# Two sums over 512 elements against one over 1024: the modulation rows on VectorE in a two-layer diffusion step

## The chip, the cores and the metric

The kernel runs on one core of a Trainium2 chip. The metric is the device time of one execution in microseconds, the median of several runs. A profile is one execution taken by the hardware profiler; its times count from the start of its span.

## What is computed

The reference takes 128 context tokens and 512 latent tokens of width 1024 through two layers. Each layer is a mixer (pooling and short convolution in layer 0, attention in layer 1) and a gated feed-forward network, and ahead of both stands a normalisation whose shift, scale and gate come from a condition vector, one for the context, one for the latents:

```python
def ada_params(cvec, w_ada, b_ada):
    m = jax.nn.silu(cvec) @ w_ada + b_ada
    return jnp.split(m[:, None, :], 6, axis=-1)

def modulate(x, g, shift, scale):
    return rms_norm(x, g) * (1 + scale) + shift

for l in range(DEPTH):
    sh1, sc1, g1, sh2, sc2, g2 = ada_params(cond, w_ada[l], b_ada[l])
    h = modulate(x, norm_g[l, 0], sh1, sc1)
    x = x + g1 * mixer(h)
    h = modulate(x, norm_g[l, 1], sh2, sc2)
    x = x + g2 * swiglu(h, w_ffn_in[l], w_ffn_out[l])
```

For each layer `ada_params` is a product of the two conditions, after a SiLU, with a matrix of 1024 by 6144. The result is 6144 modulation values for each condition and layer, which the kernel calls rows: 128 of them, one for each partition, make a block, so there are 48 blocks for each layer.

## The kernel before, in words

Everything is kept transposed: features on the 128 partitions, the 640 tokens along the free axis. All large products run on TensorE as three products of a high and a low part (`block_mm`, line 287, two halves of 320 tokens each). The low parts are made by VectorE: `pair` rounds on ScalarE (L142) and subtracts on VectorE (L143), for weights (`wl_...`, 128x1024) and for activations (`al`, `bl`).

The modulation values of layer 0's first norm, and some others, are made by TensorE (`ada_pe`). The other 84 blocks are made on VectorE by the class `AdaDve`. For one block it loads the 128 rows of the transposed matrix (`rawa`, 128x1024), and for each of the two conditions multiplies them by that condition (`silb`, the same on all partitions) and sums along the row. Before the change this is done in two halves of 512 elements, by one operation each (L365), which writes the products to a tile that nobody reads (`junk`, one buffer) and the sum to one column of `got`. So a block costs four such operations. The profile shows each as two instructions: the operation itself (CUSTOM_DVE_ANT_0) and a read of its sum (DVE_READ_ACCUMULATOR2_ANT). When a group of four or eight blocks is done, one addition (L379) joins the two halves and `ada_done` adds the bias (L386).

The order of the work. The startup, up to about 60 us, is in an order written out by hand (`manual_schedule`): two calls `ada.run(2)`, so four blocks, stand there on VectorE's queue with one weight split between them (`ws.split(2)`), ahead of the end of the first normalisation (`rsqrt_of`, L448 to L460), for which TensorE then waits. Behind it come, in this order:

- the input projection of layer 0 (`pi`, 16 products, the last 13 with `each=` calling `ada.run` for two, one or no blocks), with the pooled branch (GpSimd sums at L878, VectorE at L888 and L889), the convolution (L935 to L969) and the evacuation of each product (L505, then L510 on ScalarE, which frees the PSUM tile);
- the output projection (`po`, 8 products, one block each), with the residual update of x (L490), the operand of the next norm (`prep`, L467 on ScalarE and L469 on VectorE) and the sum of squares (L422 on ScalarE, added on GpSimd at L424); at its end `rsqrt_of` splits the sum (`bl<-ssq_a`) and TensorE reduces it (L453);
- the feed-forward network of layer 0 (`fi`, `fo`), one block for each product until all 84 are done, at 612 us;
- layer 1, which has no such blocks.

Outside the startup a planner with a model of costs puts each engine's instructions in order before the run, and at run time each engine takes them strictly in that order. The sums are kept behind what stands before them in the program (`keep_in_program_order`), but others may be put between them. GpSimd adds tensors in the stages up to 245 us; both it and VectorE read them from SBUF. All loads go through SyncE's queue, a block's rows as one transfer of 512 KB, up to six ahead.

Of the kernel before, what the change touches and what calls it, by code (L numbers as in the profile page):

```python
# [9 lines left out]
F32 = mybir.dt.float32  # L10
F32R = mybir.dt.float32r
AF = mybir.ActivationFunctionType
ALU = mybir.AluOpType
AX = mybir.AxisListType

P = 128
D = 1024
# [41 lines left out]
def hybrid_step(  # L59
# [23 lines left out]
    V, S, G, PE = nc.vector, nc.scalar, nc.gpsimd, nc.tensor  # L83
# [18 lines left out]
    def tmp(name):  # L102
        return tpool.tile([P, UL], F32, tag="t", name=name)
# [233 lines left out]
    class AdaDve:  # L337
# [13 lines left out]
        def run(self, rows, hold=True):  # L351
            for _ in range(rows):
                if self.at == len(self.todo):
                    return
                l, b0, n, b = self.todo[self.at]
                if not self.raw:
                    self.load()
                raw = self.raw.pop(0)
                self.at += 1
                if b == 0:  # L360
                    self.got = p1.tile([P, 8, 2, 2], F32, tag="got", bufs=2, name=f"got_{l}_{b0}")
                for c in range(2):
                    for q in range(2):
                        cols = slice(512 * q, 512 * q + 512)
                        op = V.tensor_tensor_reduce(  # L365
                            out=junk,
                            in0=raw[:, cols],
                            in1=silb[:, c, cols],
                            scale=1.0,
                            scalar=0.0,  # L370
                            op0=ALU.mult,
                            op1=ALU.add,
                            accum_out=self.got[:, b, c, q : q + 1],
                        )
                        if hold:
                            tc.keep_in_program_order(op)
                if b == n - 1:
                    two = self.got[:, 0:n]
                    V.tensor_tensor(out=two[:, :, :, 0], in0=two[:, :, :, 0], in1=two[:, :, :, 1], op=ALU.add)  # L379
                    ada_done(l, b0, two[:, :, :, 0])  # L380
                self.load()

    def ada_done(l, b0, got):

        n = got.shape[1]
        V.tensor_tensor(  # L386
            out=mod[l][:, b0 : b0 + n, :],
            in0=got,
            in1=sm[:, S_BA + 48 * l + b0 : S_BA + 48 * l + b0 + n, None].broadcast_to((P, n, 2)),
            op=ALU.add,  # L390
        )
        part, k0 = divmod(b0, 8)
        if part in (1, 4):
            g0 = S_NG + 8 * (2 * l + part // 3) + k0
            V.scalar_tensor_tensor(
                out=sc[l, part // 3][:, k0 : k0 + n, :],
                in0=mod[l][:, b0 : b0 + n, :],
                scalar=1.0,
                in1=sm[:, g0 : g0 + n, None].broadcast_to((P, n, 2)),
                op0=ALU.add,  # L400
                op1=ALU.mult,
            )
        known.add((l, part, k0 + n))
# [319 lines left out]
    nc.sync.dma_start(sm, small)  # L723
    with tc.tile_pool(name="pool1", bufs=1) as p1:
        silb = p1.tile([P, 2, D], F32, tag="silb", name="silb")
        junk = p1.tile([P, 512], F32, tag="junk", name="junk")
        ada_raw = []

        def ada_load(ch):
# [297 lines left out]
    with tc.tile_pool(name="pool2", bufs=1) as p2:  # L1027
# [14 lines left out]
        for dst, srcd, nm in ((kt, ckT, "ck"), (vt, cv, "cv")):  # L1042
            raw = tmp(f"raw_{nm}")
# [511 lines left out]
```

## Time and profile before

| | |
|---|---|
| median of 3 runs | 1409.69 us (1408.79 to 1410.6) |
| the profiled execution | 1408.83 us, its span 1406.9 |
| mean granted TensorE clock | 0.983 |
| sums on VectorE (L365) | 336, together 250.5 us, the last at 612 us |
| reads of their sums | 336, 81 ns each |
| additions of the halves (L379) | 11 |
| loads of rows | 84 of 512 KB, 3.5 us from issue to landing |

Rows of the profile give a line, an engine and an operation, then the tile written and the tiles read, with their shapes; "idle before" names what ended the engine's wait. TensorE's busy time is modelled from pipelined matmuls. A granted clock of 1.00 is full speed; the other state seen here is 0.50, so that a mean of 0.82 over 5 us means that 36% of it ran at half speed. The span is the time from the first to the last instruction of the execution.

### The profile page before, as it was taken

Reading aid. Unit: us, or ns where it says so; the run is one execution under the profiler, and the core shown is the slowest. Engines: PE = TensorE matmul, PEld = TensorE weight load, DVE = VectorE, ACT = ScalarE, POOL = GpSimd, SP = SyncE. Lnnn points to the kernel's source line nnn. Section 1 sums busy time; section 2 is a strip of 40 time slices with the busy share of each in tenths; the row PEclk is TensorE's granted clock in tenths of the full one; section 3 lists DMA queues with packets and bytes.
Section 4 is the critical chain, followed back from the end, with each engine's and each line's share of the span. In section 5 each row is a group of like instructions: output and inputs, shape, how many; then the busy total and the mean of one; then the engine's idle time right before and its main releaser. Section 6 shows DMA issues by size and latency. Waiting matters only on the chain.

```text
span 1406.9 us, 22549 instructions
## 1 busy us (share of the span) xinstructions
PE 1361.5 (97%) x9139; PEld 1332.9 (95%) x9139; DVE 1006.5 (72%) x1955; ACT 578.1 (41%) x1025; POOL 148.4 (11%) x116
## 2 busy tenths in 40 slices
PE   6989998999999999999999999999999999999995
PEld 3889998999999999999999899999999999999995
DVE  4899999777768787754667677778973477536745
ACT  3433334332112221232465676547652255414543
POOL 3351112000000000000203221020000000000003
PEclk7999999999999999999999999999999999999998
DMA  9634544434343534221232111012132122311212
GB/s 363 248 106 153 184 150 157 152 135 165 135 165 122 176 123 168 87 90 46 91 110 93 46 46 39 31 44 77 41 111 91 32 89 90 121 61 61 76 46 75
DMA packets 36728, 154.50 MB, mean 110 GB/s; under 512 B 3984, under 2 KB 11152, under 8 KB 26000
## 3 DMA queue, kind: packets, MB, share of 16 engines
q1 hardware_dynamic: 36624, 153.07, 31.2%
q8 instruction: 71, 1.16, 0.3%
q14 instruction: 33, 0.27, 0.1%
HBM read 147.55 MB, written 2.88 MB: 107 GB/s over the span
## 4 chain that ended last, share of the span: by engine, by line
PE 78%; DVE 16%; issue 2%; ACT 2%; DMA 1%; POOL 1%; SPq 0%; DVEq 0%; POOLq 0%; ACTq 0%
PE fi L287 26%; PE fo L287 21%; PE fi L610 16%; DVE junk L365 6%; PE pq L287 5%; PE wa L287 2%; DVE al L469 2%; PE o L1289 2%; PE s L1239 1%; DVE wl_in L143 1%; PE t L1272 1%; DVE x L490 1%; DVE wl_out L143 1%; DVE bl L143 1%; DMA raw_ada<-wada 1%
## 5 line engine op out<-in xcount | busy, mean ns | idle before, releaser
L365 DVE CUSTOM_DVE_ANT_0 junk<-rawa,silb 128x512 f32<-128x512 f32 x336 | 250.5, 746 | 7.6 <-ACT silb L793 1.0
L287 PE MATMUL fi<-al,wh_fi 128*128 128x320 f32 x832 | 192.2, 312 | 2.2 <-DVE al L469 2.2
L287 PE MATMUL fi<-ah,wh_fi 128*128 128x320 f32 x832 | 192.5, 313 | 1.4 <-ACT ah L467 1.4
L287 PE MATMUL fi<-ah,wl_fi 128*128 128x320 f32 x832 | 191.6, 312 | 0.0
L490 DVE SCALAR_TENSOR_TENSOR x<-fo,mod,x 128x128 f32<-128x128 f32 (+1 forms) x144 | 54.6, 433 | 136.5 <-PE fo L287 133.1
L287 PEld LDWEIGHTS fi<-al,wh_fi 128*128 128x128 f32 x832 | 141.7, 190 | 2.8 <-DVE al L469 2.8
L287 PEld LDWEIGHTS fi<-ah,wh_fi 128*128 128x128 f32 x832 | 141.7, 191 | 1.6 <-ACT ah L467 1.6
L287 PEld LDWEIGHTS fi<-ah,wl_fi 128*128 128x128 f32 x832 | 141.4, 190 | 0.0
L142 ACT ACTIVATE wh_fi<-raw_fi 128x1024 fp32r<-128x1024 f32 x52 | 55.0, 1058 | 172.0 <-PE fi L287 134.8
L142 ACT ACTIVATE wh_fi_p<-raw_fi 128x512 fp32r<-128x512 f32 x126 | 77.3, 627 | 111.8 <-PE fi L610 65.0
L142 ACT ACTIVATE wh_fo<-raw_fo 128x1024 fp32r<-128x1024 f32 (+1 forms) x48 | 47.5, 991 | 180.5 <-PE fo L287 132.6
L143 DVE TENSOR_TENSOR wl_fi_p<-raw_fi,wh_fi_p 128x512 fp32r<-128x512 f32 x126 | 85.6, 688 | 48.5 <-ACT wh_fi_p L142 48.2
L610 PE MATMUL fi<-bh,wl_fi_p 128*128 128x320 f32 x288 | 88.9, 309 | 0.0
L610 PE MATMUL fi<-bh,wh_fi_p 128*128 128x320 f32 x288 | 88.7, 308 | 0.0
L610 PE MATMUL fi<-bl,wh_fi_p 128*128 128x320 f32 x288 | 88.3, 307 | 0.0
L287 PE MATMUL fo<-bh,wh_fo 128*128 128x320 f32 x352 | 80.6, 310 | 0.0
L287 PE MATMUL fo<-bh,wl_fo 128*128 128x320 f32 x352 | 80.5, 310 | 0.0
L287 PE MATMUL fo<-bl,wh_fo 128*128 128x320 f32 x352 | 80.4, 310 | 0.0
L424 POOL TENSOR_TENSOR ssq_b<-ssq_b,sq_b 128x640 f32<-128x640 f32 x14 | 25.2, 1801 | 516.6 <-ACT sq_b L422 516.5
L287 PE MATMUL fo<-al,wh_fo 128*128 128x320 f32 x328 | 75.1, 310 | 0.0
L287 PE MATMUL fo<-ah,wh_fo 128*128 128x320 f32 x328 | 74.9, 309 | 0.0
L287 PE MATMUL fo<-ah,wl_fo 128*128 128x320 f32 x328 | 74.8, 309 | 0.0
(342 smaller groups left out, 3317.1 us busy)
## 6 DMA issues: line engine op xcount, KB each, us to landing
raw_fi<-wfi SPq DMA_DIRECT2D x44, 1024.0 KB, 4.8
rawa<-wada SPq DMA_DIRECT2D x84, 512.0 KB, 3.5
raw_fo<-wfo SPq DMA_DIRECT2D x16, 1024.0 KB, 4.9
raw_ada<-wada SPq DMA_DIRECT2D x12, 512.0 KB, 9.3
raw_in<-win SPq DMA_DIRECT2D x6, 1024.0 KB, 6.4
raw_fo<-wfo SPq DMA_DIRECT2D x8, 768.0 KB, 4.2
raw_qkv<-wqkv SPq DMA_DIRECT2D x6, 1024.0 KB, 4.8
raw_out<-wout SPq DMA_DIRECT2D x4, 1024.0 KB, 4.8
```

Source lines behind the costliest of these rows:

```text
L142: S.activation(h, src, AF.Copy)
L143: eng.tensor_tensor(out=l, in0=src, in1=h.bitcast(F32), op=ALU.subtract)
L287: PE.matmul(ps[:, h, 0 : hi - lo], w[a][:, k, cols], rhs[b][:, k0 + k, lo:hi], start=k == 0 and a == b, stop=k == kn - 1 and a == 1,)
L365: op = V.tensor_tensor_reduce(out=junk, in0=raw[:, cols], in1=silb[:, c, cols], scale=1.0, scalar=0.0, op0=ALU.mult, op1=ALU.add, accum_ou ...
L424: (eng or G).tensor_tensor(out=self.acc[:, cols], in0=self.acc[:, cols], in1=sq[:, cols], op=ALU.add)
L469: V.scalar_tensor_tensor(out=lo[:, k, a:b], in0=x[:, k, a:b], scalar=s[:, k, c : c + 1], in1=h[:, k, a:b].bitcast(F32), op0=ALU.mult, op1= ...
L490: V.scalar_tensor_tensor(out=xs, in0=got[:, 0 : b - a], scalar=mod[l][:, gate0 + m, c : c + 1], in1=xs, op0=ALU.mult, op1=ALU.add,)
L610: PE.matmul(out, w[a][:, k, :], ops.get(OPERAND[p], b)[:, k, :], start=fresh and k == 0 and a == b, stop=k == ops.kn - 1 and a == 1, skip_ ...
L1239: PE.matmul(self.ps[:, hf, 0:HT], bufB[a][:, self.h, q0 : q0 + P], kt[b][:, self.kv, hf * HT : hf * HT + HT], start=n == 0, stop=n == 2,)
L1272: PE.transpose(flat(pt)[:, s * P : s * P + P], self.pe[:, s * P : s * P + P], ident)
L1289: PE.matmul(po[:, 0 : 2 * P], vt[a][:, self.kv, s * P : s * P + P], got[b][:, s, :], start=s == 0 and n == 0, stop=s == 4 and n == 2,)
```

## The change

Each block and condition is summed by one operation over all 1024 elements, where there were two over 512. So `got` has one column for each block and condition, the addition of the halves is gone, and `junk` is twice as wide, 4 KB on each partition where it had 2. The number of blocks, their order in the program and their loads are unchanged.

```diff
                 if b == 0:
-                    self.got = p1.tile([P, 8, 2, 2], F32, tag="got", bufs=2, name=f"got_{l}_{b0}")
+                    self.got = p1.tile([P, 8, 2], F32, tag="got", bufs=2, name=f"got_{l}_{b0}")
                 for c in range(2):
-                    for q in range(2):
-                        cols = slice(512 * q, 512 * q + 512)
-                        op = V.tensor_tensor_reduce(
-                            out=junk,
-                            in0=raw[:, cols],
-                            in1=silb[:, c, cols],
-                            scale=1.0,
-                            scalar=0.0,
-                            op0=ALU.mult,
-                            op1=ALU.add,
-                            accum_out=self.got[:, b, c, q : q + 1],
-                        )
-                        if hold:
-                            tc.keep_in_program_order(op)
+                    op = V.tensor_tensor_reduce(
+                        out=junk,
+                        in0=raw,
+                        in1=silb[:, c, :],
+                        scale=1.0,
+                        scalar=0.0,
+                        op0=ALU.mult,
+                        op1=ALU.add,
+                        accum_out=self.got[:, b, c : c + 1],
+                    )
+                    if hold:
+                        tc.keep_in_program_order(op)
                 if b == n - 1:
-                    two = self.got[:, 0:n]
-                    V.tensor_tensor(out=two[:, :, :, 0], in0=two[:, :, :, 0], in1=two[:, :, :, 1], op=ALU.add)
-                    ada_done(l, b0, two[:, :, :, 0])
+                    ada_done(l, b0, self.got[:, 0:n])
                 self.load()
...
-        junk = p1.tile([P, 512], F32, tag="junk", name="junk")
+        junk = p1.tile([P, D], F32, tag="junk", name="junk")
```

## The prediction

> **What bounds the kernel now.** I read the page first: the span, the busy shares, the chain that ended last. Then the windows, to see where TensorE loses time, and the waits of TensorE in the stretch where it does.
>
> ```profile
> span 1406.9 us, 22549 instructions
> PE 1361.5 (97%) x9139; PEld 1332.9 (95%) x9139; DVE 1006.5 (72%) x1955; ACT 578.1 (41%) x1025; POOL 148.4 (11%) x116
> PE fi L287 26%; PE fo L287 21%; PE fi L610 16%; DVE junk L365 6%; PE pq L287 5%; PE wa L287 2%; DVE al L469 2%; PE o L1289 2%; PE s L1239 1%; DVE wl_in L143 1%; PE t L1272 1%; DVE x L490 1%; DVE wl_out L143 1%; DVE bl L143 1%; DMA raw_ada<-wada 1%
> ```
>
> TensorE is busy for 97% of the span, so at most 45 us (1406.9 less 1361.5) of pure idling, plus what a halved clock costs, could ever be won. But the sums of line 365 are the largest item of VectorE on the chain, 6%. So there is a stretch in which VectorE sets the pace. The windows show which (columns: stretch, length, then busy time and count for PE, PEld, DVE, ACT, POOL, then the granted clock).
>
> ```profile
> 80.00:100.00 20.00, 14.22 (x82) 13.96 (x81) 20.00 (x41) 7.13 (x13) 9.48 (x9) 0.83 0.30 100
> 100.00:150.00 50.00, 50.00 (x337) 49.80 (x336) 49.52 (x98) 18.25 (x30) 11.56 (x14) 1.00 0.53 178
> 160.00:165.00 5.00, 2.57 (x13) 2.31 (x12) 5.00 (x14) 1.68 (x2) 0.00 (x0) 0.82 0.40 119
> 165.00:170.00 5.00, 5.00 (x30) 5.00 (x29) 4.90 (x12) 1.12 (x2) 0.00 (x0) 0.83 0.68 270
> 235.00:240.00 5.00, 2.23 (x8) 1.45 (x9) 4.96 (x9) 3.58 (x6) 2.53 (x1) 0.83 0.23 80
> 240.00:245.00 5.00, 5.00 (x20) 5.00 (x21) 4.93 (x14) 2.90 (x7) 0.00 (x0) 0.50 0.40 131
> 245.00:612.00 367.00, 367.00 (x2476) 367.00 (x2476) 278.76 (x617) 93.17 (x142) 0.00 (x0) 1.00 0.40 141
> ```
>
> From 245 to 612 us, where more than half of the sums lie, TensorE is never idle, its clock is 1.00, and VectorE has 88 us (367 less 278.76) to spare. A saving there is worth nothing. Before 245 us VectorE is full (49.52 of 50 us, 20.00 of 20) and TensorE keeps up only by using what lies ready in its buffers; when these are empty it stops. It does so at three places:
>
> ```profile
> PE pi L287 <- ACT ev L510: 5.8, 1, 5.8
> PE pi L287 <- DVE wl_in L143: 2.4, 1, 2.4
> PE ms_a L453 <- ACT bh L142: 1.6, 1, 1.6
> PE fi L287 <- ACT ah L467: 1.4, 1, 1.4
> PE fi L287 <- DVE al L469: 0.7, 1, 0.7
> ```
>
> I call the first stop A (84 to 90 us, 5.8), the second B (160 to 163 us, 2.4) and the last three together C (234 to 239 us, 3.7). Each is followed by a slow clock, and that costs as much again: around B, 5 us at 0.82 and 5 at 0.83 lose 0.9 + 0.85 = 1.75 us, around C 0.85 + 2.5 = 3.35, of which some 0.4 fell inside the last wait, so 3.0.
>
> **The cost of one sum.** The rows of VectorE by shape give the durations, and the chain that ended last, in order of time (start, length up to the next step, what), gives what one instruction really holds the queue for.
>
> ```profile
> L365 DVE CUSTOM_DVE_ANT_0 junk<-rawa,silb 128x512 f32<-128x512 f32 x336 | 250.5, 746 | 7.6 <-ACT silb L793 1.0
> L143 DVE TENSOR_TENSOR wl_fi<-raw_fi,wh_fi 128x1024 fp32r<-128x1024 f32 x52 | 63.5, 1221 | 0.9 <-ACT wh_fi L142 0.9
> ```
>
> ```profile
> 50.51 0.69 DVE junk L365
> 51.24 0.69 DVE junk L365
> ...
> 94.19 0.60 DVE junk L365
> 94.80 0.73 DVE ev L505
> ...
> 117.70 1.14 DVE wl_in L143
> ```
>
> A sum over 512 followed by another sum takes 0.73 us from start to start (50.51 to 51.24); followed by something else only 0.61 (94.19 to 94.80): a second sum waits about 0.12 us more, I think because both write the tile junk. No row shows a sum over 1024. The nearest is a plain operation that also reads two inputs from SBUF, over 1024 elements: 1221 ns long, and it holds the queue for 1.14 us (117.70). I take 1.14 for the merged sum, 1.26 if a sum follows. Its bounds: above, the 1.47 of two sums in a row, at which nothing is won; below, 1.09, the elements alone (640 hold the queue for 0.73 at 94.80, 1024 for 1.14, so 384 more cost 0.41, 1.07 ns each). A pair of old sums then gives back 0.08 us where both stood apart (2 x 0.61 less 1.14), 0.20 where they stood together (1.47 less 1.26): the change saves two fixed parts, not half the work.
>
> How many pairs lie where (the count of sums in each stretch; columns: stretch, length, busy and count, granted clock):
>
> ```profile
> 35.00:71.00 36.00, 16.03 (x16) 1.00 0.70 251
> 71.00:89.20 18.20, 8.21 (x9) 0.97 0.14 46
> 89.20:162.60 73.40, 45.62 (x55) 0.96 0.47 158
> 162.60:234.00 71.40, 33.41 (x45) 0.98 0.49 170
> ```
>
> **The change, place by place.** *Startup, 8 pairs.* These stand in a row: 8 x 0.20 = 1.6 us, and the addition of the two halves goes (0.17).
>
> ```profile
> 53.44 0.17 DVE L379 TENSOR_TENSOR got<-got 128x8 f32<-128x8 f32 x1
> ...
> 54.27 0.81 PE L448 MATMUL ms_a<-ssq_a,ones 128*128 128x320 f32 x2 [1.54 <-DVE ssq_a L458]
> ```
>
> VectorE reaches the reciprocal root (L458 to L460) 1.8 us earlier. TensorE waits 1.54 us for exactly that, so 1.5 us is won, and the pooled branch behind it starts earlier by as much. Bounds: 0.8 (8 x 0.08 and 0.17) and 1.8, should some wait ahead of it shrink too.
>
> *Up to A, 4.5 pairs,* each standing alone: 4.5 x 0.08 = 0.4. A stays a stop of over 5 us with its slow clock. Bounds: 0.9 (0.20 each) and -0.5 (GpSimd, below).
>
> *Up to B, 27.5 pairs.* Between 2.2 us (0.08 each) and 5.5 (0.20 each). In the timeline 20 of the 55 sums are followed at once by a sum, from the first to the last of these:
>
> ```profile
> 112.18 0.68 DVE L365 CUSTOM_DVE_ANT_0 junk<-rawa,silb 128x512 f32<-128x512 f32 x1
> ...
> 155.38 1.93 DVE L365 CUSTOM_DVE_ANT_0 junk<-rawa,silb 128x512 f32<-128x512 f32 x1
> ```
>
> I take the middle, 3.9. That is above the 2.4 us by which the weight split is late, so B and its 1.75 us of slow clock go: 4.1. VectorE, though, is then only 3.9 less 4.1 ahead, level with TensorE.
>
> *Up to C, 22.5 pairs:* 1.8 to 4.5, middle 3.1. So against TensorE VectorE stands 2.9 us better at C than before (3.9 + 3.1 less 4.1). From this goes what the end of the stage gives back. Its last steps run over GpSimd:
>
> ```profile
> 236.12 2.53 POOL L424 TENSOR_TENSOR ssq_a<-ssq_a,sq_a 128x640 f32<-128x640 f32 x1 [4.60 <-ACT sq_a L422]
> ```
> ```profile
> 237.29 1.91 DVE L365 CUSTOM_DVE_ANT_0 junk<-rawa,silb 128x512 f32<-128x512 f32 x1
> ...
> 239.18 0.90 DVE L143 TENSOR_TENSOR bl<-ssq_a,bh 128x320 fp32r<-128x320 f32 x2
> ```
>
> A sum that meets an addition of GpSimd takes 1.91 us instead of 0.69: it waits until the addition is done, and the addition in its turn waits for the sum in front. With merged sums the addition waits 0.53 us more (1.14 less 0.61), and the split of its result stands behind a second sum that is 0.53 longer: 1.1 us. The Trainium skill, SBUF — State Buffer, section "Who interferes with whom", says that a Vector operation with two SBUF inputs and a GpSimd operation that reads SBUF shut each other out, the later one blocking until the first is done; the trace agrees (1.91 against 0.69). By that rule alone the wait is no longer in sum, only in larger pieces, and C would be as here.
>
> So C shrinks by 2.9 less 1.1 = 1.8 of its 3.7 us. Of the slow clock I let the smaller part go: what is left of C, 1.9 us, lies between the 1.54 us of the startup, after which the clock stayed at full (1.00 from 35 to 71 us), and the 2.4 of B, after which it lost 1.75. With that price 3.0 less 1.75 = 1.3 is won. Bounds for C: 0 and 3.7 + 3.0.
>
> *Everything after 245 us:* nothing, under the cover of TensorE, which is full there. If that cover were gone, the 211 sums left there (336 less the 125 counted above), some 105 pairs, would give another 8 to 21 us; nothing points to it. The loads are the same 84 in the same order.
>
> Sum: 1.5 + 0.4 + 4.1 + 1.8 + 1.3 = 9.1 us, against the profiled execution's 1408.83 (span 1406.9 and 1.9 around it). The median of the runs is 1409.69, 0.86 above that execution. 1409.69 less 9.1 is 1400.6.
>
> **The rivals.** *Half of it (0.17).* B goes, but the order in which VectorE's instructions are queued, which is planned anew from the new lengths, puts the longer sums in front of the last residual updates, and C stays as it is: 1.5 + 0.4 + 4.1 = 6.0, 1403.7. For it: the lead at C is small, 2.9 us. Against it: 45 sums before C become 22 or 23, with the same other work between them.
>
> *Only the startup (0.14).* The startup's order is written out by hand and its gain is sure; behind it the saved 0.08 us of each pair is lost in new waits. Then 1.5 + 0.4 = 1.9, 1407.8. For it: two thirds of the sums up to B already stand alone, so little is saved on each.
>
> *Slower, through GpSimd (0.12).* Place: the pooled branch up to A.
>
> ```profile
> 81.35 5.97 POOL L878 TENSOR_TENSOR s<-s 128x661 f32<-128x661 f32 x3
> ```
> ```profile
> L888 DVE TENSOR_TENSOR s<-s,kc 128x16 f32<-128x16 f32 x8 | 2.1, 303 | 2.4 <-POOL s L878 2.4
> ```
>
> These additions take 1.99 us each, because they alternate with VectorE. Each that meets a merged sum grows by 0.53; with 4 or 5 such meetings the branch is 2.6 us later, VectorE, whose order is fixed, stands still for it (it did for 2.4 us before), and A grows by 2.6 and one more piece of slow clock, 1.75. The meetings go on (the convolution's sums at L935 and L958, the squares at L424), and what they cost VectorE eats the 3.9 and 3.1 us saved behind A, so B and C stay, and C's end is 1.1 later: -1.5 + 2.6 + 1.75 + 1.1 = +3.95, 1413.6. It decides from the point where GpSimd's delay exceeds what VectorE has saved by then, 0.4 us at A. This is what the rule of the skill cited above would make of a longer sum, if it held at every meeting. Against it: only 9 sums lie up to A and the 2.4 us are all that VectorE waits for this branch.
>
> *The change doesn't do what it says (0.03):* a merged sum costs as much as two, 1409.7.
>
> **How the numbers follow.** The forecast case has 0.54: 1400.6, by its own bounds 1396.2 (1.8 + 0.9 + 4.1 + 6.7 = 13.5 less) to 1403.7, where the next case begins. A measurement of this kernel can tell about 0.2%, 2.8 us. Faster by more: the forecast and the half, 0.54 + 0.17 = 0.71. Within it: 0.14 + 0.03 = 0.17. Slower: 0.12. The range takes in the half and the startup case, 1396.2 to 1407.8, and leaves out the slower one and the tails.
>
> **What would show it.** A row of sums x168, of 1.20 to 1.25 us in the undisturbed ones, and no line for adding halves; in the waits of TensorE none of 2.4 us on wl_in near 160 us and no clock below 1.00 there; C short of 2.5 us; the stretch from 245 us to the end as long as before. I am wrong if VectorE shows new idle time on POOL before 90 us, if the wait on wl_in is only moved, or if the merged sum takes 1.4 us or more.

## The result, and the profile after

The changed kernel takes 1411.19 us (median of 20 runs, 1409.58 to 1412.65) where the kernel before took 1409.12 beside it: a ratio of 1.0014, interval 1.0008 to 1.002. It is slower by 2 us, where the forecast was 1400.6, some 9 us faster. The change is smaller than the 0.2% named as what can be told, but over 20 runs its interval leaves out 1. The profiled execution has a span of 1408.3 us, 1.4 more than before.

The sums did become what was priced. The page of the changed kernel, the share of lines on the chain that ended last and its group of sums:

```profile
PE fi L287 25%; PE fo L287 21%; PE fi L606 16%; PE pq L287 5%; DVE junk L363 4%; PE pi L287 3%; PE wa L287 2%; DVE al L465 2%; PE o L1285 2%; PE s L1235 2%; PE t L1268 1%; PE po L287 1%; DVE x L486 1%; DVE wl_in L143 1%; DMA raw_ada<-wada 1%
...
L363 DVE CUSTOM_DVE_ANT_0 junk<-rawa,silb 128x1024 f32<-128x1024 f32 x168 | 220.6, 1313 | 2.5 <-ACT silb L789 1.0
```

VectorE is busy 30 us less with the sums (220.6 against 250.5) and their share of the chain fell from 6% to 4%. What TensorE waited for between 71 and 250 us in the changed kernel:

```profile
PE pi L287 <- ACT ev L506: 10.3, 1, 10.3
PE pi L287 <- DVE wl_in L143: 2.3, 2, 2.1
PE ms_a L449 <- ACT bh L142: 2.2, 1, 2.2
PE py L901 <- ACT ev L506: 2.1, 2, 1.8
```

Stop A, 5.8 us before, is 10.3. B, 2.4 us at 160, is gone from there, but two stops of 1.8 and 2.1 us stand at 122 and 147 us, the second again on `wl_in`. C has shrunk from 3.7 to 2.2. The windows of before, asked of the changed kernel, show the same in time and clock (same columns):

```profile
80.00:100.00 20.00, 9.74 (x50) 9.47 (x49) 20.00 (x30) 5.22 (x10) 9.27 (x7) 0.74 0.36 117
100.00:150.00 50.00, 45.60 (x302) 44.54 (x301) 47.14 (x64) 20.92 (x34) 14.67 (x15) 1.00 0.48 165
160.00:165.00 5.00, 5.00 (x36) 5.00 (x35) 5.00 (x8) 1.86 (x3) 0.00 (x0) 1.00 0.52 137
...
240.00:245.00 5.00, 3.70 (x13) 3.42 (x14) 3.78 (x6) 4.22 (x9) 0.68 (x1) 0.66 0.14 38
245.00:612.00 367.00, 367.00 (x2477) 367.00 (x2476) 261.71 (x410) 93.17 (x142) 0.00 (x0) 1.00 0.40 142
```

From 80 to 100 us TensorE does 50 matmuls where it did 82. From 245 to 612 us it is full as before.

Why A grew can be read from the number of sums in each stretch (columns: stretch, length, VectorE's time in them and their count):

```profile
35.00:68.90 33.90, 13.52 (x8) 1.00 0.72 263
68.90:91.10 22.20, 11.90 (x8) 0.93 0.31 99
91.10:148.90 57.80, 31.62 (x24) 0.94 0.47 161
148.90:236.10 87.20, 34.12 (x23) 1.00 0.45 151
```

Between the split of the first pooled group (`bl<-pl`, 70.7 us before, 69.0 now) and the evacuation that ends A (`ev<-pi`, 89.2 and 91.1) stand 8 merged sums. Before there were 9 halves, that is 4.5 merged. The order of VectorE's queue shows how that came about; a stretch of its timeline before the change and after it:

```profile
76.75 0.68 DVE L365 CUSTOM_DVE_ANT_0 junk<-rawa,silb 128x512 f32<-128x512 f32 x1
...
77.36 0.81 DVE L505 TENSOR_TENSOR ev<-pi,rstd 128x640 f32<-128x640 f32 x1
78.10 0.67 DVE L365 CUSTOM_DVE_ANT_0 junk<-rawa,silb 128x512 f32<-128x512 f32 x1
...
78.70 0.81 DVE L143 TENSOR_TENSOR bl<-pl,bh 128x640 fp32r<-128x640 f32 x1
```

```profile
76.08 1.21 DVE L363 CUSTOM_DVE_ANT_0 junk<-rawa,silb 128x1024 f32<-128x1024 f32 x1
77.23 0.08 DVE L363 DVE_READ_ACCUMULATOR2_ANT got<- 128x1 f32 x1
77.23 0.81 DVE L143 TENSOR_TENSOR bl<-pl,bh 128x640 fp32r<-128x640 f32 x1
77.97 1.21 DVE L363 CUSTOM_DVE_ANT_0 junk<-rawa,silb 128x1024 f32<-128x1024 f32 x1
79.11 0.08 DVE L363 DVE_READ_ACCUMULATOR2_ANT got<- 128x1 f32 x1
79.11 0.81 DVE L501 TENSOR_TENSOR ev<-pi,rstd 128x640 f32<-128x640 f32 x1
```

One sum, another operation, one sum, another operation: so it stands here before the change, with halves, and after it, with sums of nearly twice the length. The planner went by gaps, so nearly the same gaps now hold two thirds more work. 9 halves held the queue for 5.5 us (9 x 0.61), 8 merged sums hold it for 9.1 (77.97 to 79.11 is 1.14): 3.6 us more. From `bl` to `ev` the two traces take 18.5 and 22.1 us, 3.6 us more.

GpSimd is no part of these 3.6 us. Its six additions of the pooled branch in this stretch did grow, from 11.2 us together to 13.8; the last three were 5.97 and are now:

```profile
83.60 7.06 POOL L874 TENSOR_TENSOR s<-s 128x661 f32<-128x661 f32 x3
```

But VectorE is held by them no longer than before: it shows no idle time in this stretch, and in each of the two traces seven of its operations here are longer by 1.1 to 1.35 us than elsewhere, together 7.9 us in both.

The rest of A's growth is on ScalarE, which frees the PSUM tile behind VectorE's evacuation. Its queue before and after:

```profile
88.72 0.74 ACT L142 ACTIVATE bh<-pl 128x640 fp32r<-128x640 f32 x1 [8.34 <-DVE pl L889]
90.06 0.17 ACT L510 ACTIVATE ev<-pi 128x2 f32<-128x2 f32 x1 [0.61 <-DVE ev L505]
```
```profile
91.25 0.74 ACT L142 ACTIVATE bh<-pl 128x640 fp32r<-128x640 f32 x1 [10.06 <-DVE pl L885]
91.89 1.04 ACT L142 ACTIVATE wh_in<-raw_in 128x1024 fp32r<-128x1024 f32 x1
92.83 0.15 ACT L506 ACTIVATE ev<-pi 128x2 f32<-128x2 f32 x1
```

After the change the rounding of a weight (`wh_in`) stands ahead of the operation that frees the tile, so that it starts 1.7 us behind the start of `ev` where it was 0.8. So A's 4.5 us are made of 1.7 by which TensorE comes earlier, 1.9 by which `ev` starts later, and 0.8 to 0.9 on ScalarE. Why the planner put the rounding there was not tested.

What became of the time that VectorE saved behind A: it stands idle. Its waits between 69 and 236 us in the changed kernel:

```profile
DVE x L486 <- PE po L287: 7.3, 1, 7.3
DVE bl L910 <- ACT bh L909: 2.8, 1, 2.8
DVE ev L501 <- PE pi L287: 1.9, 2, 1.6
DVE al L465 <- ACT ah L463: 0.2, 1, 0.2
```

Before, it waited for nobody in this stretch but GpSimd, for 1.2 us at its start. Now it waits 7.3 us for the output projection: it comes to that update 3.7 us earlier than before (181.03 us against 184.77), and TensorE, held at A and at the two stops behind it, begins the output projection 4.0 us later (174.9 against 170.9).

From the stops and the clock rows the difference between the two traces adds up so: TensorE reaches A 1.7 us earlier (82.8 against 84.5), A is 4.5 longer and its slow clock 0.2; 4.4 us of stops at full clock stand where B and its slow clock cost 4.1; C with its slow clock costs 3.9 instead of 6.7. Together -1.7 + 4.7 + 0.3 - 2.8 = +0.5. The first matmul of `fo`, behind all this, starts at 350.7 us where it started at 349.7, so half a microsecond is in no stop that I named. The stops at 122 and 147 us were not taken apart; in the merged kernels with a later order, below, TensorE has neither.

### The profile page after: what moved, and what is told of

Read it like the earlier page. It is cut to its first block, busy times and chain, and to the rows that moved or that the text cites. A ratio compares the mean times of both kernels' runs of the same rounds, so it can differ in the third digit from the quotient of the medians.

```text
span 1408.3 us, 22206 instructions
## 1 busy us (share of the span) xinstructions
PE 1359.5 (97%) x9139; PEld 1330.5 (94%) x9139; DVE 979.1 (70%) x1608; ACT 578.6 (41%) x1025; POOL 157.7 (11%) x116
## 4 chain that ended last, share of the span: by engine, by line
PE 82%; DVE 12%; issue 2%; ACT 2%; DMA 1%; POOL 1%; SPq 0%; DVEq 0%; ACTq 0%; POOLq 0%
PE fi L287 25%; PE fo L287 21%; PE fi L606 16%; PE pq L287 5%; DVE junk L363 4%; PE pi L287 3%; PE wa L287 2%; DVE al L465 2%; PE o L1285 2%; PE s L1235 2%; PE t L1268 1%; PE po L287 1%; DVE x L486 1%; DVE wl_in L143 1%; DMA raw_ada<-wada 1%
## 5 line engine op out<-in xcount | busy, mean ns | idle before, releaser
L363 DVE CUSTOM_DVE_ANT_0 junk<-rawa,silb 128x1024 f32<-128x1024 f32 x168 | 220.6, 1313 | 2.5 <-ACT silb L789 1.0
```

The source lines that it names most:

```text
L363: op = V.tensor_tensor_reduce(out=junk, in0=raw, in1=silb[:, c, :], scale=1.0, scalar=0.0, op0=ALU.mult, op1=ALU.add, accum_out=self.got[: ...
```

## The experiments

Two theories. *Order*: a merged sum costs what was priced, but the planned order puts more work ahead of the evacuation at A, and TensorE's lateness from there makes VectorE's saving idle. *Port*, the rival: the length of a merged sum itself is at fault, since it keeps GpSimd, and through it the pooled branch, waiting. A third possibility was that VectorE is as full as before and lateness only moves.

All times are medians; each run was timed beside the kernel before, which lay between 1409.07 and 1409.57 us. The blocks ahead of A count from the end of the startup; "last x" is the end of the last residual update of the output projection in the profile; the time of the sums is summed from each start to the next on VectorE's queue without waits for GpSimd, from the first `bl<-pl` to there.

| kernel | time, us | ratio, interval | A, us | blocks ahead of A | sums, us | VectorE idle, us | last x, us |
|---|---|---|---|---|---|---|---|
| before | | | 5.8 | 2 1/4 | 70.6 | 0 | 234.6 |
| changed | 1411.19 | 1.0014 [1.0008, 1.002] | 10.3 | 4 | 62.3 | 12.2 | 236.1 |
| with short sums | 1407.7 | 0.9992 [0.9983, 1.0] | 7.2 | 2 1/2 | 71.0 | 0 | 233.1 |
| merged in the startup only | 1407.12 | 0.9987 [0.9978, 0.9995] | 5.8 | 2 1/4 | 70.6 | 0 | 232.9 |
| merged behind the startup only | 1412.26 | 1.0018 [1.0009, 1.0027] | 10.3 | 4 | 62.4 | 12.0 | 238.2 |
| merged in the last 48 blocks only | 1409.59 | 1.0001 [0.9992, 1.001] | 5.8 | 2 1/4 | 70.6 | 0 | 234.8 |
| halves, two scratch tiles | 1417.24 | 1.0056 [1.0043, 1.0069] | 10.1 | 4 | 66.1 | 13.3 | 243.2 |
| merged, later | 1398.29 | 0.9922 [0.9908, 0.9935] | 3.1 | 1 | 64.4 | 1.7 | 224.4 |
| halves, later | 1410.17 | 1.0007 [0.9998, 1.0016] | 3.5 | 1 | 72.9 | 1.7 | 236.1 |
| merged, later still | 1395.25 | 0.9901 [0.9887, 0.9914] | 1.5 | 0 | 59.7 | 4.6 | 221.5 |
| halves, later still | 1406.64 | 0.9982 [0.9973, 0.9991] | 1.5 | 0 | 68.6 | 4.6 | 232.9 |
| merged, one step more | 1395.37 | 0.9901 [0.9887, 0.9915] | 1.5 | 0 | 59.8 | 5.5 | 221.6 |

**Merged sums with short ones between them.** The second of two sums covers 8 elements; its result is not used. The scratch tile is as wide as in the changed kernel, and the addition of the halves is left out.

```diff
-                        cols = slice(512 * q, 512 * q + 512)
+                        cols = slice(0, 8 if q else D)
...
-                    ada_done(l, b0, two[:, :, :, 0])
+                    ada_done(l, b0, self.got[:, 0:n, :, 0])
```

> Merged sums, and behind each a sum over 8 elements whose result is not used, so that VectorE's queue holds as many sums as before the change. Order theory: the planner puts one sum between two other operations whatever its length, so with the short sums in between, 5 merged and 5 short sums stand ahead of the evacuation that ends stop A (8 merged in the changed kernel, 9 halves before). 5 x 1.14 + 5 x 0.15 = 6.45 us against 5.5 before: A about 6.8 us (5.8 before, 10.3 changed); a pair costs 1.3 to 1.45 us, as two halves did, so the whole 1409 to 1410.5. Port theory (a longer sum keeps GpSimd, and so the pooled branch, waiting): the long sums are all there, A stays near 10 us and the time at 1411 or above.

TensorE's waits from 71 us on:

```profile
PE pi L287 <- ACT ev L508: 7.2, 1, 7.2
PE ms_a L451 <- ACT bh L142: 2.2, 1, 2.2
PE fi L287 <- ACT ah L465: 1.8, 1, 1.8
PE fi L287 <- DVE al L467: 0.7, 1, 0.7
```

The short sums fill every second gap, A falls back to 7.2 us and the kernel to 1407.7, 1.3 us faster than the order theory said; B is gone, for a reason not looked into. The port theory wanted A near 10 and 1411: as stated it falls. By itself this run doesn't part the two theories cleanly, since only 5 long sums stand ahead of A where 8 did. But as in the two traces above, seven operations of VectorE are lengthened by GpSimd ahead of A, and the kernel with two scratch tiles, below, has no long sum at all.

**Merged in one part only.** One condition on the block's number picks one sum or two: up to the fourth block (startup), behind it, or from the 37th on. All three have the scratch tile of the changed kernel, and only groups of halves are added; the edit of the first:

```diff
+                cuts = 1 if self.at <= 4 else 2
                 for c in range(2):
-                    for q in range(2):
-                        cols = slice(512 * q, 512 * q + 512)
+                    for q in range(cuts):
+                        n1 = D // cuts
+                        cols = slice(n1 * q, n1 * q + n1)
...
```

> Merged sums in the four blocks of the startup alone, halves behind them. Order theory: the planned order behind the startup is that of the kernel before, so everything is 1.7 us earlier, A stays 5.8, B 2.4, C 3.7: 1407.4. A theory in which merged sums cost more than their rows show (wider scratch tile, queue): 1409 or above.

> Halves in the four blocks of the startup, merged sums everywhere behind. The complement of the startup run (1407.1, 2.0 under before). Order theory: the changed kernel without its startup gain, A about 10, 1411.2 + 2.0 = 1413. If the two parts are not additive because A absorbs the startup gain: 1411.

> Halves in the first 36 blocks, merged sums in the other 48, which lie in the feed-forward network. Both theories: TensorE covers it, 1409.1, within 0.5. If the time depended on VectorE's work there, 48 x 2 x 0.08 to 0.20 us, 8 to 19 us less.

The startup alone wins about 2 us and leaves A, B and C as they were. Merging everything else alone loses 2.7, with A at 10.3 us: the loss is all in the planned part. Merging the last 48 blocks is worth nothing, TensorE covers them. The parts add up only within their noise: -2.0 + 2.7 is +0.7, each part known to about 1.2 us either way, and the changed kernel's own is +2.07, between 1.1 and 2.8. The 1412.3 lies between the two forecasts for that run, so whether A absorbs some of the startup's gain stays open.

**The changed kernel's order, with halves.** The two halves write two scratch tiles in turn; nothing else is changed.

```diff
+        junk2 = p1.tile([P, 512], F32, tag="junk2", name="junk2")
...
-                            out=junk,
+                            out=(junk, junk2)[q],
```

> The kernel before (halves), with two scratch tiles that the two halves write in turn, so that the second half need not follow the first one's write. The planner then queues them behind each other, and as many blocks stand ahead of the evacuation of stop A as in the changed kernel, 4 since the startup (16 halves), where there were 2 1/4. Order theory: no merged sum is in this kernel, and yet it is slow: A 16 x 0.61 less 9 x 0.61 = 4.3 us longer than before, about 10, less whatever the startup wins by the missing 0.12 us between sums; 1410 to 1413. Port theory, or any by which the length of a merged sum is at fault: as the kernel before or faster, 1407 to 1409.

Two sums in a row in its timeline, in the startup, and TensorE's first two waits:

```profile
47.91 0.68 DVE L365 CUSTOM_DVE_ANT_0 junk<-rawa,silb 128x512 f32<-128x512 f32 x1
48.52 0.08 DVE L365 DVE_READ_ACCUMULATOR2_ANT got<- 128x1 f32 x1
48.52 0.68 DVE L365 CUSTOM_DVE_ANT_0 junk<-rawa,silb 128x512 f32<-128x512 f32 x1
```
```profile
PE pi L287 <- ACT ev L510: 11.3, 3, 10.1
PE pi L287 <- DVE bl L915: 3.5, 1, 3.5
```

This kernel has no merged sum, its sums in a row are cheaper than before (0.61 us from start to start, 0.73 with one tile), and it is the slowest of all, 7.7 us behind the kernel before. With no common scratch tile the planner queues up to eight sums behind each other, 16 halves stand ahead of A, from `bl` to `ev` it takes 22.8 us (18.5 before, 22.1 in the changed kernel), and A is 10.1. So it is the amount of work in sums ahead of A, and the one scratch tile was what had spaced them. That it is 1417 and not 1410 to 1413 comes with a further stop of 3.5 us at 114 us, where other rows of sums stand ahead of `bl`; I had counted A alone.

**Another order, with merged sums and with halves.** The 18 blocks of the input projection are handed out later.

```diff
-            each=lambda i: ada.run(1 + (i < 7) - (i >= 11)),
+            each=lambda i: ada.run((0, 0, 1, 1, 1, 2, 2, 2, 2, 2, 2, 2, 1)[i]),
```

> The changed kernel with the 18 blocks of the input projection handed out later (0,0,1,1,1,2,2,2,2,2,2,2,1 for its 13 steps, where it was 2 x7, 1 x4, 0 x2). Order theory: one block (2 merged sums) stands ahead of the evacuation that ends A where there were four, 6.8 us less, so A is at most 3 us; the 8 us that VectorE saves up to 235 us are now of use, since A no longer hands TensorE's lateness on: 1399 to 1404, under both kernels. If instead VectorE is as full as before and only the place of its lateness moves, B or C grows by what A loses: 1409 to 1411.

> The kernel before (halves) with the same later handing out. Order theory: A shrinks below 3 us too, but VectorE has the same 164 us of work between 71 and 235 us and no idle time to give, so the lateness comes back at B or C: 1406 to 1410, and merging is worth the difference to the merged kernel of the same order, 4 to 8 us. If the handing out is all that counts, it is as fast as the merged one.

Merged, TensorE waits for this:

```profile
PE pi L287 <- ACT ev L506: 3.1, 1, 3.1
PE ms_a L449 <- ACT bh L142: 2.2, 1, 2.2
PE po L287 <- DVE bl L143: 0.6, 1, 0.6
PE po L287 <- ACT bh L142: 0.4, 1, 0.4
```

1398.3, 10.8 us under the kernel before. With halves A shrinks too, to 3.5, and nothing is won: 1410.2, the lateness comes back as 2.8, 2.0 and 1.2 us further on. Both times lie just outside what I had expected. In this order merging is worth 11.9 us, more than the 4 to 8 expected: 1.8 of them come from the startup (the first `bl<-pl` is at 69.1 us, with halves at 70.9) and 8.5 from the sums behind it (64.4 against 72.9). The third possibility, that lateness only moves, holds for the halves, whose work fills VectorE but for 1.7 us; it does not hold for the merged sums.

**Later still.** `(0, 0, 0, 1, 1, 1, 2, 2, 2, 2, 2, 2, 1)`, merged and with halves, and `(0, 0, 0, 0, 1, 1, 2, 2, 2, 2, 2, 2, 2)`, merged. Two blocks move to the feed-forward network.

> Merged sums handed out still later, 0,0,0,1,1,1,2,2,2,2,2,2,1, so two blocks fewer up to the end of the output projection. Order theory: no sum at all stands ahead of the evacuation that ends A; two sums less than in the run that was 1398.3, 2.3 us, so A goes from 3.1 to about 1 us and its slow clock (3.4 us at half, 1.7) goes too: 1394.5 to 1397. If something other than VectorE's queue holds A by now (the pooled branch on GpSimd): 1398.

> Halves, handed out as in the fastest run (0,0,0,1,1,1,2,2,2,2,2,2,1), so two blocks fewer than in the kernel before up to the end of the output projection. Order theory: VectorE has no idle time to give, so against the first late order with halves (1410.2) only those two blocks count, 8 sums of 0.65 us, 5.2 us: 1405; merging is then worth some 10 us in this order (1395.3), the 8 us of VectorE time and the slow clock behind a wait. If the order alone made the fastest run fast: 1395 to 1398.

> Merged sums, one step later still (0,0,0,0,1,1,2,2,2,2,2,2,2). Stop A has no sum ahead of it in either, so nothing is left to win there; what is late is the sum of squares over GpSimd at the end of the stage (2.2 us and its slow clock), with the same sums around it: 1395, within 1.5. A gain of 2 us or more would say that sums behind A still held TensorE.

1395.25 us, the fastest: 0.9901 of the kernel before, interval 0.9887 to 0.9914. In it VectorE waits for GpSimd ahead of A, and no sum stands there:

```profile
DVE s L884 <- POOL s L874: 4.6, 3, 2.8
DVE ev L501 <- POOL s L874: 1.2, 1, 1.2
```

So the pooled branch has become what ends A, and one step more brings nothing (1395.37). The halves in the same order take 1406.6, where 1405 was expected: the order alone, with its two blocks fewer in these stages, is worth about 3 us, merging in it 11.4.

## Why the prediction was wrong, point by point

- *The price of a merged sum* (1.14 us, 1.26 if a sum follows): right, 77.97 to 79.11 is 1.14. The two in a row after 46.86 lie 1.25 apart (46.86 to 48.11 us).
- *What the change gives VectorE* between the end of the startup and C: forecast 0.4 + 3.9 + 3.1 = 7.4 us, measured 8.3 (70.6 less 62.3). Right as a sum; where it would be of use was wrong.
- *The startup*, 1.5 us: right, within its bounds. TensorE reaches A 1.7 us earlier, and the kernel merged there alone is about 2 us faster. Its wait of 1.54 us is not all gone, 0.5 is left; the rest was won ahead of it, which only the upper bound had allowed for.
- *"Up to A, 4.5 pairs"*: this is the step that failed. I counted the halves that lay ahead of A and halved them, as if the order stayed. The order is planned by gaps, 8 merged sums went there, 9.1 us of work where 9 halves were 5.5, and instead of a gain of 0.4 us A grew by 4.5, of which 0.8 to 0.9 came from ScalarE's order. I had written that the order "is planned anew", but only as a cause for losing the gain at C.
- *"B goes ... 4.1"* and *"C shrinks"*: both were seen, in part. B's place is free, but a wait of 2.1 us on `wl_in` stands at 147 us: it was moved, which the prediction had named as a sign of being wrong, and with the other stops it costs 4.4. C gave back 2.8 us where 3.1 were forecast (1.8 + 1.3), and that nearness is luck in part: TensorE, held up before, ended the output projection 3.9 us later than before the change (its last matmul starts at 231.4 against 227.5), VectorE its last update only 1.5. For behind a later A TensorE, not VectorE, was late, and 12.2 us of VectorE's time went idle, 7.3 of it in one wait for the output projection. In the order with one block ahead of A a gain of the forecast's size was there: 1398.3, inside the range.
- *GpSimd at the end of C*, 1.1 us: half right. The addition took 3.05 us where it took 2.53, as priced, and TensorE waited 2.2 for the split where it waited 1.6. But no second sum stood ahead of the split this time: VectorE was idle there for 1.9 us until ScalarE had rounded the sum.

```profile
237.63 3.05 POOL L420 TENSOR_TENSOR ssq_a<-ssq_a,sq_a 128x640 f32<-128x640 f32 x1 [3.67 <-ACT sq_a L418]
```

- *The rival "slower, through GpSimd"* named the right place, A, and the wrong mechanism, and its 1413.6 is near the measured time by luck. GpSimd's additions did grow by the 2.6 us that it gave, but they held VectorE no longer than before between `bl` and `ev` (7.9 us in both traces); the sums in its own queue held the evacuation. The run with two scratch tiles, as slow at A without a merged sum, tells these apart.
- *Everything after 245 us*, nothing: right (1409.59 beside 1409.57 with only those blocks merged).

## What to carry to other kernels

When filler work is made coarser and another hand (a planner, a fixed pattern of gaps) decides where it goes, count what then stands ahead of each operation that frees something, not only what the filler costs in sum: fewer and longer pieces in the same gaps are more work ahead of it (here 8 of 1.14 us in place of 9 of 0.61). A saving on an engine that another engine waits for is only had if the first stop of that other engine does not grow. And an order should be tried together with the finer or coarser work, since here neither won much by itself (2 us lost, 3 us won) and both together 14.

## What the runs showed of the hardware

Two sums in a row that write the same scratch tile start 0.73 us apart, with two scratch tiles 0.61: I had only supposed that the common tile was the reason, and the 0.12 us is its price here.

The slow clock does not go by the length of a stop alone. In the changed kernel the stops of 1.8 us at 122 and 2.1 at 147 left the granted clock at 1.00, as did the 1.5 us at A in the fastest kernel, while the 2.2 us at the end of C brought a piece of half clock (0.66 from 240 to 245 us), as the 2.4 at B had. A shorter stop did so too, in the kernel with halves handed out later still: 1.95 us, and then 0.66 from 225 to 230 us.

```profile
224.51 0.42 PE L287 MATMUL fi<-ah,wh_fi 128*128 128x322 f32 x1 [1.95 <-DVE ah L482]
```
```profile
225.00:230.00 5.00, 5.00 (x25) 5.00 (x24) 4.97 (x8) 2.66 (x4) 2.54 (x1) 0.66 0.63 199
```

The Trainium skill, TensorE: Matmul & The Clock Gate, section "Why this matters for your kernels", asks for no gaps over about 3 us; the traces do not bear that limit out, since 1.95, 2.2 and 2.4 us were enough. What else decides was not tested.
